# Seven block products for eight in the input projection: Strassen's scheme for keys, queries, values and gates of all tokens, and for conv of the first 768

## The chip, the cores and the metric

The kernel runs on one core of a Trainium2 chip, in one launch. The metric is the device time of one execution in microseconds. The runs of the kernel before have a median of 1464.25 us (1463.36 to 1465.06, three runs).

## The reference, cut to what matters

One layer of a streaming encoder: an input projection to eight groups of 512 columns, a gated short convolution, attention over a band of nine chunks of 64 tokens, an output projection, a gated embedding. All is float32; 2048 prompt tokens and 32 sample tokens go through the same weights.

```python
z = rmsnorm(x, norm_in) @ w_in                # (2080, 1024) @ (1024, 4096)
h, bg, cg, zc, q, k, v, za = split(z, 512)
u  = cg * h
yc = bg * (w[0]*u[t-2] + w[1]*u[t-1] + w[2]*u[t]) * silu(zc)
ya = softmax(q @ k_band.T / 8 + bias) @ v_band * silu(za)     # 8 heads of 64
x  = x + concat(rmsnorm(yc), rmsnorm(ya)) @ w_out
x  = x + sigmoid(rmsnorm(x) @ w_ple_gate) * (p @ w_ple_proj)
return rmsnorm(x), and the newest keys, values and conv rows
```

## The kernel before, in words

**Precision.** Every matrix factor is split into a high part, rounded to the fast float32 format, and a low part, the rest. A product is three matmuls: high by high, high by low, low by high (`products`, L279 to L281; conv has its own copy at L1085). A split is one ACT copy for the high part and one DVE subtraction for the low part.

**Tokens and weights.** The 2080 tokens, normalised and transposed (features on partitions), stay on the chip as `Xh` and `Xl`, in five chunks of 256, 384, 512, 512 and 416 tokens. The 4096 columns of `w_in` come in 16 slots of 256 columns: keys, queries, values, gates (`a`), then eight slots of conv pairs (h with C, B with z). Weights of a slot are loaded to `RAW`, split into `WS` (two sets) while the slot before is multiplied.

**First stage.** For each slot and chunk, `block` makes 24 matmuls (8 k-blocks by 3) into one of five PSUM banks in turn. Keys and queries are split and stored to HBM (`split_store`, L294 to L299), gates go through Silu. Values are made token-major, with tokens as the stationary side, 128 tokens at a time (`values`), so they need no transposes. Of the newest keys token-major rows are wanted too: `key_rows` puts their transposes in a list, `held`, and `release` emits them after the next block. Background work (caches, `w_out` and the two embedding weights, split and stored to `wd`) is done two pieces at a time behind a chunk. Stores are staged in `hi_r` and `lo_r`, three buffers of 512 columns each.

**Conv.** Eight slots for the first pass over tokens (chunks 0 and 1), whose split weights are also stored to `wc`. The passes over chunks 2, 3 and 4 load them again; their matmuls are the dense work between which the pieces of attention are put (`dense`, `attention`, one piece whenever the share of dense columns done passes the share of pieces).

**Output stage.** Output projection, embedding, final norm, per 128 tokens; weights loaded from `wd` in blocks.

All order is written out by hand: each engine runs its instructions in the order of the code, SP issues nearly all DMAs in that order, ACT the loads of background work.

## Time and profile before

| | |
|---|---|
| median of the runs | 1464.25 us |
| profiled execution: its own time | 1465.2 us |
| its span, first to last instruction | 1463.2 us |
| busy: PE, DVE, ACT, POOL | 97%, 42%, 37%, 21% |
| first stage (keys, queries, values, gates) | 11.5 to 400.3 us |
| conv, first pass | 400.3 to 515 us |
| conv with attention | 515 to 1016 us |
| output stage | 1016 to 1463.2 us |

The span is what the queries of the trace count in; about 2 us of the time lie outside it. PE's durations of single matmuls overlap, so what one costs is seen in the distance between starts. A busy time counts an engine only while it computes: waiting and issuing DMAs are left out.

### The profile page before, as it was taken

The numbers are of one execution on the slowest core, as the hardware profiler recorded it, in microseconds if no ns is written. First come the engines' busy times: TensorE is split into PE (matmuls) and PEld (weight loads), VectorE is DVE, ScalarE is ACT, GpSimd is POOL, SyncE is SP. The second block draws the span as 40 slices with busy tenths as digits, with TensorE's granted clock in tenths as the row PEclk, the third lists the DMA queues.
The fourth block names the chain that finished last, engine by engine and source line by source line (L and its number), as shares of the span: only waits on it lengthen the run. The fifth ranks groups of instructions, "written<-read, shape, count | busy, mean of one in ns | idle before, by whom it ended". The sixth has DMA issues, their size and how long they took to land.

```text
span 1463.2 us, 22734 instructions
## 1 busy us (share of the span) xinstructions
PE 1426.2 (97%) x8362; PEld 1269.9 (87%) x8362; DVE 609.4 (42%) x1346; ACT 543.5 (37%) x1182; POOL 314.0 (21%) x438
## 2 busy tenths in 40 slices
...
GB/s 222 196 109 198 294 314 312 292 286 149 79 249 260 213 183 180 159 163 122 170 174 195 126 148 270 251 231 232 363 102 69 72 48 93 48 80 40 60 25 33
DMA packets 176391, 249.10 MB, mean 170 GB/s; under 512 B 19564, under 2 KB 124816, under 8 KB 170136
## 3 DMA queue, kind: packets, MB, share of 16 engines
...
## 4 chain that ended last, share of the span: by engine, by line
PE 86%; DMA 5%; DVE 3%; issue 2%; ACT 2%; SPq 1%; POOL 1%; POOLq 0%; DVEq 0%; ACTq 0%
PE PS L1085 20%; PE PS L279 17%; PE PS L280 16%; PE PS L281 16%; PE PS L546 5%; PE PS L664 3%; PE PS L618 3%; DMA GR<-wd 2%; PE PS L662 1%; PE PS L871 1%; DMA GR<-qs 1%; PE PS L829 1%; PE PS L268 1%; DMA GF<-ext 1%; DVE GF L1099 1%
## 5 line engine op out<-in xcount | busy, mean ns | idle before, releaser
L279 PE MATMUL PS<-GR 128*128 128x512 f32 (+3 forms) x1336 | 476.2, 356 | 2.9 <-DVE GF L1120 1.8
L280 PE MATMUL PS<-GR 128*128 128x512 f32 (+3 forms) x1336 | 471.9, 353 | 1.1 <-DVE GR L271 0.6
L281 PE MATMUL PS<-GR 128*128 128x512 f32 (+3 forms) x1336 | 471.9, 353 | 0.5 <-DVE GR L812 0.5
L1085 PE MATMUL PS<-GR 128*128 128x512 f32 (+3 forms) x1920 | 432.1, 361 | 0.6 <-DMA GR<-wc 0.6
L1085 PEld LDWEIGHTS PS<-GR 128*128 128x128 f32 x1920 | 310.8, 191 | 16.8 <-DMA GR<-wc 0.9
L279 PEld LDWEIGHTS PS<-GR 128*128 128x128 f32 x1336 | 253.2, 190 | 34.2 <-DVE GF L1120 2.1
L281 PEld LDWEIGHTS PS<-GR 128*128 128x128 f32 x1336 | 253.1, 189 | 31.6 <-DVE GR L812 1.0
L280 PEld LDWEIGHTS PS<-GR 128*128 128x128 f32 x1336 | 253.4, 190 | 30.9 <-DMA GR<-wd 1.1
L578 POOL TENSOR_SCALAR GF<-GF,SM 128x640 f32<-128x640 f32 (+3 forms) x132 | 98.5, 746 | 265.7 <-DVE SM L572 195.8
L593 DVE TENSOR_TENSOR GR<-PS,GR 128x256 fp32r<-128x256 f32 (+2 forms) x184 | 103.2, 562 | 98.9 <-ACT GR L592 98.7
L592 ACT ACTIVATE GR<-PS 128x256 fp32r<-128x256 f32 (+2 forms) x184 | 89.8, 489 | 78.4 <-PE PS L618 76.7
L1107 POOL TENSOR_TENSOR GF<-GF 128x512 f32<-128x512 f32 (+3 forms) x20 | 22.4, 1122 | 409.1 <-DVE GF L1106 408.4
L566 ACT ACTIVATE GF<-GF,SM 128x640 f32<-128x640 f32 (+3 forms) x132 | 99.9, 757 | 22.7 <-DVE SM L558 21.4
L558 DVE CUSTOM_DVE_ANT_0 GF<-PS,GF 128x640 f32<-128x640 f32 (+3 forms) x132 | 96.2, 729 | 24.7 <-PE PS L546 20.8
L546 PE MATMUL PS<-GR 128*128 128x320 f32 (+6 forms) x512 | 94.9, 307 | 11.7 <-DMA GR<-qs 7.4
L546 PEld LDWEIGHTS PS<-GR 128*128 128x128 f32 x512 | 81.4, 190 | 20.9 <-issue 7.7
L910 DVE TENSOR_TENSOR GF<-PS,GF 128x512 f32<-128x512 f32 (+2 forms) x35 | 23.6, 675 | 176.3 <-ACT GF L909 176.3
L909 ACT ACTIVATE GF<-PS,SM 128x512 f32<-128x512 f32 (+2 forms) x35 | 23.6, 675 | 163.9 <-PE PS L281 82.7
L664 PE MATMUL PS<-GR 128*128 128x256 f32 x448 | 78.0, 289 | 3.0 <-DVE GR L593 3.0
L195 DVE SCALAR_TENSOR_TENSOR GR<-GF,cT,GR 128x256 fp32r<-128x256 f32 x112 | 45.8, 480 | 73.9 <-ACT GR L194 73.9
L912 POOL TENSOR_TENSOR GF<-GF 128x512 f32<-128x512 f32 (+1 forms) x32 | 41.1, 1285 | 159.7 <-DVE GF L910 141.5
L671 ACT ACTIVATE GF<-PS 64x256 f32<-64x256 f32 (+1 forms) x72 | 26.0, 360 | 130.7 <-PE PS L664 124.2
...
## 6 DMA issues: line engine op xcount, KB each, us to landing
GR<-wc SPq DMA_DIRECT2D x32, 1024.0 KB, 7.3
GR<-wd SPq DMA_DIRECT2D x72, 256.0 KB, 6.8
...
wc<-GR SPq DMA_DIRECT2D x16, 1024.0 KB, 7.6
GR<-qs SPq DMA_DIRECT2D x128, 128.0 KB, 3.2
wd<-GF SPq DMA_DIRECT2D x50, 256.0 KB, 6.1
...
vd<-GF SPq DMA_DIRECT2D x40, 256.0 KB, 5.1
```

What stands on the lines that cost most here:

```text
L195: dve.scalar_tensor_tensor(wl[:, k], RAW[:, k], cT[:, k:k + 1], wh[:, k].bitcast(F32), ALU.mult, ALU.subtract)
L279: pe.matmul(out, wh(k), xh(k), start=(k == ks_[0]), stop=False)
L280: pe.matmul(out, wh(k), xl(k), start=False, stop=False)
L281: pe.matmul(out, wl(k), xh(k), start=False, stop=(k == ks_[-1]))
L546: pe.matmul(ps[:, e, c:c + n_], q[h][b][:, qa], K[h][:, r:r + n_], start=(b == 0 and c == 0), stop=(b == 1), skip_group_check=True)
L558: dve.tensor_tensor_reduce(pr.rearrange("p (b c) -> p b c", b=nb), ps, br.rearrange("p (b c) -> p b c", b=nb), 1.0, 3e38, ALU.add, ALU.min ...
L566: act.activation(pr, pr, AF.Exp, bias=mx[rows], scale=-1.0, accum_out=sm[rows])
L578: pool.tensor_scalar(pr, pr, rs[rows], 1.0, ALU.mult, ALU.mult)
L592: act.activation(dst_of(hi), src, AF.Copy)
L593: dve.tensor_tensor(dst_of(lo), src, dst_of(hi).bitcast(F32), ALU.subtract)
L664: pe.matmul(PS[:, PS_AV, 0:256], v(k), t[:, slot_of[k], :], start=(i == 0), stop=(i == len(both) - 1))
L1085: pe.matmul(ps, a[:, k, js], b[c][:, k, :], start=(k == i == 0), stop=(k == KT - 1 and i == 2))
```

## The change

**The scheme.** For a slot of 256 columns and a pass of 2n tokens, the weights are a 2 by 2 of blocks A (column half by k half) and x a 2 by 2 of blocks B (k half by token half). Strassen's scheme in Winograd's form makes the four result blocks from seven block products, each 12 matmuls (4 k-blocks by 3) of n columns, instead of eight. The factors are A11, A12, A22 and four sums S1 to S4 of weight quarters on one side; B11, B21, B22 and four differences T1 to T4 on the other (`XP`). All seven on each side are split into high and low. The products are steps 0 to 6 of a slot: steps 0, 2, 4, 6 use one PSUM bank, X, and 1, 3, 5 another, Y. ACT copies the first product out after step 0 (L472); DVE adds make U2 after step 1, U4 after step 3 and the blocks C22, C12, C21 after steps 4, 5, 6; step 2 leaves the fourth block, C11, in PSUM.

**Passes.** Three passes over tokens (`PARTS`): 768 to 1535 (n = 384), 1536 to 2079 (n = 272), 0 to 767 (n = 384). Each goes through the eight slots of keys, queries, values and gates: slots 0 to 23. Weights are loaded, summed and split anew in each pass. Slots 24 to 31 are conv for the last pass, tokens 0 to 767. For the other 1312 tokens x is stored, split, to `xd` (`keep_x`), and loaded again as three chunks of 480, 432 and 400 tokens for the conv under attention, which makes 24 matmuls a block as before.

**What goes with it.** Values come out with features on partitions and are transposed. x is no longer on the chip as a whole, only the pass's seven pieces; the pieces of the next pass are split during the eighth slot of a pass. Weight pieces lie in a ring of ten. Staging of stores is one ring, `hl_r`, of three buffers that hold high and low parts (768 columns). Background work is taken one piece at a time, up to three in a slot, after steps 1, 3, 5 (`work_one`), loads after steps 0, 2, 4; none in slots 7, 8, 9, 12, 13 and 23. The first slots' steps are interleaved with the preparation of x.

**Values and newest keys on PE**, in slot 8 (keys of tokens 1536 to 2079; before: keys of chunk 3). Names: PS is PSUM, GR and GRa hold split factors, GF staging, ident the identity of a transpose. Before, around the transposes of one block:

```order
L279 MATMUL PS<-GR 128x512
L280 MATMUL PS<-GR 128x512
L281 MATMUL PS<-GR 128x512
L313 MATMUL PS<-ident,GF 128x128
L279 MATMUL PS<-GR 128x512
L280 MATMUL PS<-GR 128x512
```

Now:

```order
L374 MATMUL PS<-ident,GF 128x128
L374 MATMUL PS<-ident,GF 112x128
L374 MATMUL PS<-ident,GF 32x128
L466 MATMUL PS<-GRa 128x272 x12
L374 MATMUL PS<-ident,GF 128x128
L374 MATMUL PS<-ident,GF 112x128
L374 MATMUL PS<-ident,GF 32x128
```

The transposes (L313, now L374) stood behind the 24 matmuls of the next block; now they stand behind the 12 of the step that makes their block, ahead of the next step, and values have them too.

**Background work and stores on ACT**, in a slot of queries (slot 3; before: the second slot of queries). L294 and L351 write high parts of queries, L336 and L540 those of cache values, L376 those of background weights, L244 those of weights of the next slot, L283 evacuates transposed x; DMA rows load background work. Before:

```order
L294 ACTIVATE GR<-PS 128x416
L294 ACTIVATE GF<-PS 128x416
L336 ACTIVATE GF<-GF 128x4x64 x4
L371 DMA GF<-in_w_out_dram 128x512 x2
L294 ACTIVATE GF<-PS 128x256
L294 ACTIVATE GR<-PS 128x256
L376 ACTIVATE GF<-GF,cT 128x512 x2
L371 DMA GF<-in_w_out_dram 128x512 x2
L294 ACTIVATE GR<-PS 128x384
L294 ACTIVATE GF<-PS 128x384
```

Now:

```order
L283 ACTIVATE ST<-PS,cT 128x128 x4
L244 ACTIVATE GRa<-GF 128x512
L540 ACTIVATE GF<-GF 128x4x64 x2
L351 ACTIVATE GF<-GF 128x384
L244 ACTIVATE GRa<-GF 128x512
L534 DMA GF<-in_cache_v_dram 128x512
L351 ACTIVATE GF<-GF 128x384
L244 ACTIVATE GRa<-GF 128x512
L540 ACTIVATE GF<-GF 128x4x64 x2
L351 ACTIVATE GF<-GF 128x384
L244 ACTIVATE GRa<-GF 128x512 x2
L266 ACTIVATE PS,SM<-ST 128x1024
```

The stores' high parts stood in groups of two to four, each with a PSUM bank of five; now single ones alternate with background work and weight splits, all through the one staging ring.

**The start on DVE**: before, from the first normalised tiles to the first store; now, from the low part of the second piece of x (B21) to that of T2. L209 and L245 make low parts of weights, L271 and L285 evacuate transposed x, L269 normalises, L315 makes low parts of x pieces, L309 differences of x blocks; ST holds x. Before:

```order
L257 TENSOR_SCALAR GF<-GF,SM 128x1024 x2
L209 SCALAR_TENSOR_TENSOR GR<-GF,cT,GR 128x128 x4
L271 TENSOR_TENSOR GR<-PS,GR 128x4x128 x2
L209 SCALAR_TENSOR_TENSOR GR<-GF,cT,GR 128x128 x2
L271 TENSOR_TENSOR GR<-PS,GR 128x4x128 x2
L209 SCALAR_TENSOR_TENSOR GR<-GF,cT,GR 128x128 x2
L246 COPY cT<-PS 128x36
L209 SCALAR_TENSOR_TENSOR GR<-GF,cT,GR 128x128 x8
L295 SCALAR_TENSOR_TENSOR GF<-PS,GF 128x256
```

Now:

```order
L315 TENSOR_TENSOR GRa<-ST,GRa 128x1536
L285 TENSOR_SCALAR ST<-PS,cT 128x128 x4
L245 TENSOR_TENSOR GRa<-GF,GRa 128x512
L269 TENSOR_SCALAR GF<-GF,SM 128x1024
L245 TENSOR_TENSOR GRa<-GF,GRa 128x512
L285 TENSOR_SCALAR ST<-PS,cT 128x128 x4
L269 TENSOR_SCALAR GF<-GF,SM 128x1024
L285 TENSOR_SCALAR ST<-PS,cT 128x128 x4
L309 TENSOR_TENSOR GF<-ST 128x1536
L309 TENSOR_TENSOR ST<-ST,GF 128x1536
L245 TENSOR_TENSOR GRa<-GF,GRa 128x512
L315 TENSOR_TENSOR GRa<-ST,GRa 128x1536
```

Evacuated x was split at once (L271); now it is evacuated whole, and the splits and differences of 1536 elements follow as instructions of their own.

The diff, cut to its core:

```diff
-CHUNKS = [(0, 256), (256, 384), (640, 512), (1152, 512), (1664, 416)]
+PARTS = [(768, 384), (1536, 272), (0, 384)]
+CHUNKS = [(768, 480), (1248, 432), (1680, 400)]
...
-PASSES = [(0, 1), (2, 3), (4,)]
+PASSES = [(0, 1), (2,)]
...
-    hi_r = Ring([G(4132, 512), G(5156, 512), R(O_SP, 512).bitcast(F32)])
-    lo_r = Ring([G(4644, 512), G(5668, 512), R(O_SP + 512, 512).bitcast(F32)])
...
-    psm = Ring([0, 1, 2, 3, 4])
...
+    XP = ["B11", "T2", "B21", "T1", "T3", "B22", "T4"]
+    hl_r = Ring([G(6400 + 768 * i, 768) for i in (2, 0, 1)])
...
+    def sums(q):
...
+        tt(S1, quad(raw, 1, 0), quad(raw, 1, 1), ALU.add)
+        tt(S2, S1, quad(raw, 0, 0), ALU.subtract)
+        tt(S3, quad(raw, 0, 0), quad(raw, 1, 0), ALU.subtract)
+        tt(S4, quad(raw, 0, 1), S2, ALU.subtract)
+
+    def split_w(q, *pieces):
...
+        for i in pieces:
+            hi, lo = piece(q, i)
+            act.activation(hi, src[i], AF.Copy)
+            (pool if i in (4, 5) else dve).tensor_tensor(lo, src[i], hi.bitcast(F32), ALU.subtract)
...
+    def combine(p, name, on=pool):
+
+        a, b = {"T1": ("B12", "B11"), "T2": ("B22", "T1"), "T3": ("B22", "B12"),
+                "T4": ("B21", "T2")}[name]
+        on.tensor_tensor(xsource(p, name), xsource(p, a), xsource(p, b), ALU.subtract)
+
+    def split_x(p, name, on=dve):
+        hi, lo = xpiece(p, XP.index(name))
+        src = xsource(p, name)
+        act.activation(hi, src, AF.Copy)
+        on.tensor_tensor(lo, src, hi.bitcast(F32), ALU.subtract)
...
+    def step(q, i, use, mid=None):
...
+        ps = (X, Y, X, Y, X, Y, X)[i]
...
+        for k in range(4):
+            for m, (a, b) in enumerate(((wh, xh), (wh, xl), (wl, xh))):
+                pe.matmul(ps, a[:, k], b[:, k], start=(first and k == m == 0),
+                          stop=(k == 3 and m == 2), skip_group_check=True)
+            if mid and k == 1:
+                mid()
+        c = lambda t: t[:, 0:n]
+        if i == 0:
+            act.activation(c(t1_of(q)), X, AF.Copy)
+        elif i == 1:
+            dve.tensor_tensor(c(U2), Y, c(t1_of(q)), ALU.add)
+        elif i == 2:
+            use(q, 0, 0, X)
+        elif i == 3:
+            dve.tensor_tensor(c(U4), Y, c(U2), ALU.add)
+        else:
+            out, base, a, j, e = ((C22, U4, X, 1, 1), (C12, U2, Y, 0, 1), (C21, U2, X, 1, 0))[i - 4]
+            dve.tensor_tensor(c(out), a, c(base), ALU.add)
+            use(q, j, e, c(out))
...
+    def token_major(src, p, e, use):
...
+        def later():
+            pt = PS[:, pst()].rearrange("p (a b) -> p a b", a=4)
+            for m, (o, w, _) in enumerate(got):
+                pe.transpose(pt[0:w, m], src[:, o:o + w], ident)
...
+        held.append(later)
...
+    split_x(0, "B11")
+    sums(0)
+    norm_x(9, dve)
+    step(0, 0, take)
+    split_x(0, "B21")
+    tr_x(9)
...
+    combine(0, "T1", dve)
+    combine(0, "T2", dve)
+    split_w(0, 1)
+    split_x(0, "T2")
+    later.pop(0)()
+    constants(cst2, 8, 36)
+    step(0, 1, take)
...
+    def prepare_w(q, i):
+
+        if i == -1:
+            sums(q)
+            split_w(q, 0, 2)
+        elif i == 1:
+            split_w(q, 1, 3)
+        elif i == 3:
+            split_w(q, 6)
+            if NQ <= q < len(SLOTS):
+                keep_w(q)
+            load_raw(q + 1)
+        elif i == 4:
+            split_w(q, 4)
+        elif i == 5:
+            split_w(q, 5)
...
+    def kqva_slot(q):
...
+        for i in range(7):
+            if (q, i) in done:
+                continue
+            step(q, i, take, mid.get(i))
+            release()
+            if s8 == 7 and p < 2:
+                t = XP[i]
+                split_x(p + 1, t)
+                if t in ("B11", "B21", "B22"):
+                    keep_x(p + 1, t)
+                if t == "B21":
+                    combine(p + 1, "T4")
+            prepare_w(q + 1, i)
...
+            if not busy:
+                if i in (1, 3, 5) and len(loaded) == 2:
+                    work_one()
+                if i in (0, 2, 4):
+                    load_one()
```

795 lines of the change are left out of this document (476 added, 319 removed).

## The prediction, made before the change had been run

> **What bounds the kernel now.** I read the page first (busy time, chain), then busy time by stage, then single matmuls.
>
> ```profile
> span 1463.2 us, 22734 instructions
> PE 1426.2 (97%) x8362; PEld 1269.9 (87%) x8362; DVE 609.4 (42%) x1346; ACT 543.5 (37%) x1182; POOL 314.0 (21%) x438
> ...
> PE 86%; DMA 5%; DVE 3%; issue 2%; ACT 2%; SPq 1%; POOL 1%; POOLq 0%; DVEq 0%; ACTq 0%
> ...
> ```
>
> TensorE is busy for 97% of the span and holds 86% of the chain of waits. The next view cuts the span at the places where the program changes; its columns are length, busy time of PE, PEld, DVE, ACT and POOL, granted clock, DMA share and GB/s.
>
> ```profile
> 11.50:400.30 388.80, 387.15 (x2413) 361.42 (x2413) 122.38 (x244) 144.88 (x315) 29.68 (x47) 1.00 0.66 222
> 400.30:515.00 114.70, 114.70 (x779) 114.33 (x778) 42.38 (x100) 33.83 (x81) 7.32 (x11) 1.00 0.68 239
> 515.00:1016.00 501.00, 480.32 (x3098) 429.33 (x3097) 280.05 (x748) 232.86 (x566) 141.87 (x216) 0.99 0.55 186
> 1016.00:1463.20 447.20, 435.80 (x2032) 357.22 (x2030) 160.39 (x243) 124.78 (x205) 132.61 (x154) 0.99 0.27 88
> 150.00:250.00 100.00, 100.00 (x639) 94.50 (x638) 35.88 (x68) 32.48 (x67) 0.00 (x0) 1.00 0.90 310
> ```
>
> The first row is keys, queries, values and gates: 387.15 of 388.80 us of TensorE. The second is conv of the first 640 tokens, the third the rest of conv under attention, the fourth the output stage, which the change leaves alone. In the first two nothing but TensorE matters: DVE and ACT are busy for under 40%, so they may come late without being felt. In the last row, 100 us out of the first stage, DMA is at 0.90 of its time with 310 GB/s and TensorE never waits. So a matmul removed is worth its interval, as long as the others keep up. The price of one is the distance from start to start, not its duration. Single matmuls in order of time (first and last of 14 rows, of 12, of 11):
>
> ```profile
> 20.28 0.28 PE L280 MATMUL PS<-GR 128*128 128x256 f32 x1
> ...
> 21.84 0.28 PE L281 MATMUL PS<-GR 128*128 128x256 f32 x1
> ...
> 34.10 0.33 PE L279 MATMUL PS<-GR 128*128 128x384 f32 x1
> ...
> 36.00 0.34 PE L281 MATMUL PS<-GR 128*128 128x384 f32 x1
> ```
>
> ```profile
> 55.82 0.39 PE L280 MATMUL PS<-GR 128*128 128x512 f32 x1
> ...
> 58.08 0.39 PE L281 MATMUL PS<-GR 128*128 128x512 f32 x1
> ```
>
> So 256 columns cost 1.56/13 = 0.120 us, 384 cost 1.90/11 = 0.173, 512 cost 2.26/10 = 0.226. On the lines between: 272 columns 0.127, 400 0.180, 416 0.186, 432 0.193, 480 0.213.
>
> **The products removed.** Before, a 128-column block of the projection over all tokens is 24 x (0.120 + 0.173 + 2 x 0.226 + 0.186) = 22.3 us; twelve for keys, queries and gates make 269, values (17 tiles x 48 x 0.120) 98: 367 us. Now 24 slots (8 column pairs in 3 passes) have 84 matmuls each: 672 x (0.173 + 0.127 + 0.173) = 318. That is **-49**. Conv's eight Strassen slots take 672 x 0.173 = 116 where the old first pass took 384 x (0.120 + 0.173) = 112.5: **+4** there; but they cover 768 tokens instead of 640, and what is left under attention is 384 x (0.213 + 0.193 + 0.180) = 225 for 384 x (2 x 0.226 + 0.186) = 245: **-20**.
>
> **Transposes and the places where TensorE now waits.** Values now come out feature-major, so each block is transposed: 72 transposes, at
>
> ```profile
> 46.42 0.87 PE PS L268 x8
> ```
>
> 0.87/8 = 0.11 us each: **+8**. They are emitted directly behind the step that makes the block, not one block later as the key transposes were. TensorE runs in order, so it waits there for the DVE add (or ACT copy) and the hand-over. 24 such places in values and 8 in keys, 0.56 us for the add (the 128x384 row below) plus 0.1: **+21**. Below nothing is excluded, since step and transposes depend on each other; above it is whatever DVE is late.
>
> ```profile
> L194 ACT ACTIVATE GR<-GF,cT 128x256 fp32r<-128x256 f32 x112 | 46.2, 497 | 8.8 <-DMA GF<-in_w_in_dram 8.8
> ...
> L195 DVE SCALAR_TENSOR_TENSOR GR<-GF,cT,GR 128x256 fp32r<-128x256 f32 x112 | 45.8, 480 | 73.9 <-ACT GR L194 73.9
> ...
> L912 POOL TENSOR_TENSOR GF<-GF 128x512 f32<-128x512 f32 x30 | 38.6, 1286 | 155.1 <-DVE GF L910 140.3 <-issue 14.7
> ...
> L812 DVE TENSOR_TENSOR GR<-GR 128x1024 fp32r<-128x1024 f32 x16 | 19.6, 1223 | 13.4 <-ACT GR L811 12.1
> ...
> L592 ACT ACTIVATE GR<-PS 128x128 fp32r<-128x128 f32 x16 | 4.3, 266 | 0.0
> ...
> L295 DVE SCALAR_TENSOR_TENSOR GF<-PS,GF 128x384 fp32r<-128x384 f32 x5 | 2.8, 557 | 8.5 <-ACT GF L294 8.5
> ...
> L376 ACT ACTIVATE GF<-GF 128x512 fp32r<-128x512 f32 x3 | 1.9, 627 | 0.5 <-DMA wd<-GF 0.5
> ```
>
> **The start.** Before:
>
> ```profile
> 1.17 4.53 DMA GF<-in_x_prompt_dram
> 5.78 1.16 ACT GF L255 x2
> ...
> 7.29 0.92 POOL SM L144
> ...
> 8.91 1.13 DVE GR L209 x4
> 10.04 1.20 DVE GR L271 x2
> ...
> 12.42 0.38 PE PS L280
> ```
>
> First tile after 5.7 us, first product near 12, then almost no gap. Now step 1 needs three whole token tiles, and four steps (8.3 us of TensorE) can run before T2, which needs all six tiles. Until T2's low part DVE has 6 normalisations and 24 evacuations, 4 weight parts, 2 differences of 1536 and 3 low parts of 1536. At 1.22 for 1024 elements, 0.27 for 128 (ACT's row, taken for DVE too), 0.61 for 512 and 1.83 for 1536 (the 1024 row halved, and by one and a half) that is 7.3 + 6.5 + 2.4 + 9.2 = 25 us, behind the first normalisation at 8.2: 33 at the earliest. Following the queues (the last tiles land behind 5 MB; ACT's squares stand behind its own splits) I get 43. Then each of the next steps needs on DVE an add, a low part for the store, a weight part and a 1.83 us split: 0.56 + 0.56 + 0.61 + 1.83 = 3.6 us and a hand-over against 2.1 of TensorE, so slot 0 ends near 65. Slot 1 adds five weight parts and the storing of B12: 80. TensorE's own work to there is 12 + 29 + 5 = 46; less the 2 us lost before, **+32** (bounds +20 and +40).
>
> **The slots with background work.** This decides. A slot of 384 columns has 84 x 0.173 = 14.5 us of products, of 272 10.7. Every store of keys, queries, gates, values and prepared weights goes through one ring of three staging buffers, written by ACT, then DVE, freed when the store has landed. A slot with three pieces of background work uses it 4 + 6 = 10 times. A use lasts 0.50 (ACT, 256 columns) + 0.48 (DVE) + 0.4 (SP's issue) + landing:
>
> ```profile
> wd<-GF SPq DMA_DIRECT2D x50, 256.0 KB, 6.1
> ...
> GF<-in_w_in_dram SPq DMA_DIRECT2D x6, 1024.0 KB, 6.5
> ...
> kd<-GF SPq DMA_DIRECT2D x12, 192.0 KB, 2.1
> ```
>
> 2.1 us landing gives 3.5 a use, 10/3 x 3.5 = 11.6 a slot, hidden; 6.1 gives 7.5 and 25 us. A loaded slot moves 1.05 (weights) + 0.5 (x) + 1.6 + 1.6 (stores) + 0.8 MB = 5.5 MB, in 18 us 305 GB/s: what the 150 to 250 stretch moves, where the 6.1 belongs; but there stores went out in groups of four to eight, here three at most. I take 4.0: 5.4 a use, **18 us** a slot. By DMA alone 5.5 MB at 310/0.90 GB/s are 16.0, so the slot is over 14.5 in any case. ACT waits in order for the buffer; behind it stand the copy of the first product and the weight splits, and TensorE has two PSUM banks, one step of slack (2.1 us), where it had five. So: six key, query and gate slots of 384 columns (slots 2, 3, 16 to 19) +19 together, value slots 4, 5, 20 +3 (their waits hide most), slot 6 with a flush +5, slots 10, 11, 14 of 272 columns (8 to 12 uses against 11) +13, slot 15, where DVE also has seven splits of 1.8, +7, slot 7 +2: **+49**. The four sums of weight quarters and two low parts, 6 x 1.29 = 7.7 us on POOL, lie beside 10.7 or more; uncovered they would cost the rest of 7.7. Loading weights (6.5 us for 1 MB) lies beside the last three steps.
>
> **Under attention**, the 20 us of dense work saved count nearly in full, TensorE being busy 480 of 501 us, and
>
> ```profile
> L546 PE MATMUL PS<-GR 128*128 128x128 f32 x48 | 10.8, 253 | 7.4 <-DMA GR<-qs 7.4
> ```
>
> the 7.4 us that the first scores waited for queries go, as their load now stands a slot earlier; chunk 1 of x, loaded behind the last slot, gives half of it back: **-24** with the 20.
>
> **Sum**, against the profiled execution's 1465.2 (span 1463.2): -49 + 4 + 8 + 21 + 32 + 49 - 24 = +41, 1506. The median of the runs is 1 lower: **1505 us**.
>
> **The clock.** When TensorE stood still for 2.2 us, the clock was granted at 0.51 for the next 3.5 us:
>
> ```profile
> 774.90:777.10 2.20, 0.00 (x0) 0.00 (x0) 1.97 (x6) 0.00 (x0) 0.00 (x0) 1.00 0.00 0
> 777.70:781.20 3.50, 3.50 (x11) 2.71 (x10) 0.92 (x3) 1.43 (x4) 1.63 (x3) 0.51 0.13 41
> ```
>
> Stalls of 2 us in fourteen slots would cost up to 14 x 1.7 = 24 us; I leave that to the upper bound, since a slot's stall is spread over several steps. [...]
>
> **Rivals.** (1) *Stores land as quietly as the 2.1 us of keys*: the ring never fills, the +49 goes, 1456. For it: only three stores are out at a time; against: the bytes per slot. [...] This case is faster; it turns at a landing of about 3 us. (2) *TensorE stays the only bound*, start and waits hidden too: 1465 - 49 + 4 - 24 + 8 = 1404. For it: DVE and ACT are below 45% on average; against: the start has no other work. (3) *Landing at 6.1, and the clock falls at the stalls*: 25 us for ten loaded slots and more in the short ones, +85 on the forecast at the end, 1550 in its middle. (4) Start and waits just eat what the products save: 1465. That the products are not made fewer is excluded: the program has 84 a slot.
>
> **Chances.** Forecast (1475 to 1535) 0.57; rival 1 0.15, rival 2 0.06, rival 3 0.17, rival 4 0.05 (its higher half counts as the same). Range 1435 to 1555: it takes in rival 1 and most of rival 3, and leaves out rival 2 and the tail of 3. A change within 0.2% cannot be told from none here: faster 0.22, same 0.03, slower 0.75.
>
> **What would show it.** TensorE busy below 85% between 80 us and the last gate slot; ACT's longest waits on stores of weights, keys and queries; loaded slots of 384 columns 17 to 20 us long, against 14.5 to 16 in conv's slots; the first product on T2 after 33 us; the first dense matmul of conv near 580 us (now 515). If loaded slots take 15 to 16 us, the ring was priced wrong and rival 1 holds; if slot 1 ends before 60 us, the start was.

## The result, and the profile after

The changed kernel takes **1753.26 us** (median of four runs, 1750.91 to 1754.42) against 1464.28 of the kernel before in the same rounds: 1.197 times as long (95% interval 1.195 to 1.199). The forecast was 1505, with 1555 as its upper end: slower as said, but by 289 us instead of 41.

The head of the page and the first line of the chain of waits of the changed kernel:

```profile
span 1752.6 us, 23444 instructions
PE 1467.5 (84%) x8102; PEld 1318.3 (75%) x8102; DVE 903.5 (52%) x1669; ACT 679.7 (39%) x1465; POOL 631.0 (36%) x640
...
PE 53%; DMA 10%; DVE 6%; issue 5%; ACT 4%; POOL 2%; SPq 1%; ACTq 0%; DVEq 0%; POOLq 0%
```

TensorE held 86% of the chain and holds 53% now. It has 260 matmuls fewer, but is busy for 41 us more. The next view says why: busy time by stage (slots 0 and 1; slots 2 to 23; conv's Strassen slots up to the first dense matmul; conv with attention; output stage), columns as in the prediction.

```profile
23.30:121.10 97.80, 54.34 (x202) 47.56 (x203) 52.62 (x62) 33.85 (x62) 33.79 (x25) 0.67 0.35 118
121.10:668.00 546.90, 371.71 (x2041) 351.45 (x2040) 318.34 (x482) 232.90 (x528) 239.52 (x173) 0.85 0.60 185
668.00:810.60 142.60, 128.92 (x675) 122.91 (x674) 89.26 (x115) 43.46 (x80) 73.74 (x54) 0.93 0.69 223
810.60:1300.00 489.40, 462.58 (x3109) 429.60 (x3107) 275.10 (x747) 234.18 (x568) 141.09 (x221) 0.99 0.60 201
1300.00:1752.60 452.60, 439.85 (x2028) 358.25 (x2028) 160.18 (x243) 123.97 (x205) 133.84 (x154) 0.99 0.26 87
```

In the first two rows the granted clock is 0.67 and 0.85, where it was 1.00. In stretches granted 0.50, 259 us long in all before the dense conv, TensorE is busy for 158 us; a step's 12 products, 2.1 us at 0.173 each, took 4.21 us in one of them (from 65.37 us). So its busy time grows. Nobody else is full either: of 546.9 us DVE is busy for 58%, ACT for 43%, POOL for 44%, DMA at 0.60. It is a stage in which everyone waits for someone. Against the forecast's times: slots 0 and 1 end at 121 us (80 was said, +41); slots 2 to 23 take 547 (580 less 80 less 116 of conv: 384, +163); conv's slots 142 (116, +26); the rest 943 (the 948 of before less 24, +19). Together that is, to a microsecond of rounding, the whole error of 248. (Conv's slots end here at the first dense matmul, at 810.5 us; the expectations count that point some 3 us earlier, as 807.)

TensorE's groups in these stages, with what ended its idle time; L472 is the copy of the first product, L474 the add of U2, L314 a high part of x, L481 the adds of C22, C12, C21:

```profile
L466 PE MATMUL PS<-GRa 128*128 128x384 f32 (+1 forms) x2688 | 528.4, 358 | 174.1 <-ACT GF L472 95.4 <-DVE GF L474 21.5 <-ACT GRa L314 18.6
...
L374 PE MATMUL PS<-ident,GF 128*128 128x128 f32 (+3 forms) x96 | 19.1, 313 | 50.1 <-DVE GF L481 42.6 <-ACT GF L441 6.9 <-issue 0.6
```

The products waited 174 us, most for the copy; the transposes 50, where the forecast had 21. One of the waits for the copy, in slot 17 ahead of its third step, in order of time. SP's rows are DMA issues; what stands in brackets is how long the engine had been idle, and for whom:

```profile
507.62 0.37 SPq L204 DMA_DIRECT2D GF<-in_w_in_dram  x1
508.62 2.22 SPq L508 DMA_DIRECT2D wd<-GF  x2
...
516.21 0.52 ACT L351 ACTIVATE GF<-GF 128x384 fp32r<-128x384 f32 x1 [4.16 <-DMA wd<-GF]
...
518.55 0.51 ACT L504 ACTIVATE GF<-GF,cT 128x256 fp32r<-128x256 f32 x1 [0.50 <-DMA kd<-GF]
...
519.09 1.19 DVE L505 SCALAR_TENSOR_TENSOR GF<-GF,cT 128x256 fp32r<-128x256 f32 x1 [0.21 <-ACT GF L504]
...
520.20 0.55 DVE L481 TENSOR_TENSOR GF<-PS,GF 128x384 f32<-128x384 f32 x1
520.83 0.52 ACT L351 ACTIVATE GF<-GF 128x384 fp32r<-128x384 f32 x1 [1.77 <-DVE GF L481]
521.26 0.61 ACT L244 ACTIVATE GRa<-GF 128x512 fp32r<-128x512 f32 x1
...
522.30 0.47 ACT L472 ACTIVATE GF<-PS 128x384 f32<-128x384 f32 x1
...
522.82 1.01 PE L466 MATMUL PS<-GRa 128*128 128x384 f32 x2 [5.30 <-ACT GF L472]
```

Read it upwards. TensorE waits 5.30 us for the copy. Ahead of the copy on ACT stand weight splits (L244) and the store of C21 (L351), which waits for DVE's add, which stands behind DVE's low part of background work (L505), which waits for ACT's high part (L504). That one waited half a microsecond for a staging buffer, and stands on ACT behind the store of the block before (L351 at 516.21), which had waited 4.16 us for one: that buffer came free when a store of background weights landed, over 7 us after its issue, with the load of 1 MB of weights issued 1 us ahead of it. Which of these links carries the time is what the runs ask.

### The profile page after: what moved, and what is told of

It is laid out like the page before. It is cut to its first block, busy times and chain, and to the rows that moved or that the text cites. A ratio compares the mean times of both kernels' runs of the same rounds, so it can differ in the third digit from the quotient of the medians.

```text
span 1752.6 us, 23444 instructions
## 1 busy us (share of the span) xinstructions
PE 1467.5 (84%) x8102; PEld 1318.3 (75%) x8102; DVE 903.5 (52%) x1669; ACT 679.7 (39%) x1465; POOL 631.0 (36%) x640
## 4 chain that ended last, share of the span: by engine, by line
PE 53%; DMA 10%; DVE 6%; issue 5%; ACT 4%; POOL 2%; SPq 1%; ACTq 0%; DVEq 0%; POOLq 0%
PE PS L1401 10%; PE PS L466 8%; PE PS L1161 7%; PE PS L1160 7%; PE PS L1159 7%; PE PS L882 4%; PE PS L1000 3%; PE PS L954 2%; DMA wd<-GF 2%; DMA qs<-GF 2%; PE PS L998 1%; DMA GRa<-wd 1%; DVE GRa L245 1%; DMA kd<-GF 1%; PE PS L1214 1%
## 5 line engine op out<-in xcount | busy, mean ns | idle before, releaser
L466 PE MATMUL PS<-GRa 128*128 128x384 f32 (+1 forms) x2688 | 528.4, 358 | 174.1 <-ACT GF L472 95.4
L466 PEld LDWEIGHTS PS<-GRa 128*128 128x128 f32 x2688 | 494.2, 213 | 195.5 <-ACT GF L472 100.7
L245 POOL TENSOR_TENSOR GRa<-GF,GRa 128x512 fp32r<-128x512 f32 x64 | 86.4, 1351 | 337.7 <-ACT GRa L244 337.7
L1401 PE MATMUL PS<-GRa 128*128 128x432 f32 (+1 forms) x768 | 189.5, 366 | 0.4 <-DMA GRa<-wc 0.4
L245 DVE TENSOR_TENSOR GRa<-GF,GRa 128x512 fp32r<-128x512 f32 x160 | 164.3, 1057 | 33.2 <-ACT GRa L244 32.9
L1160 PE MATMUL PS<-GRa 128*128 128x512 f32 (+1 forms) x440 | 170.3, 387 | 1.0 <-DMA GRa<-wd 1.0
L1159 PE MATMUL PS<-GRa 128*128 128x512 f32 (+1 forms) x424 | 164.1, 387 | 1.8 <-DMA GRa<-wd 1.3
L1161 PE MATMUL PS<-GRa 128*128 128x512 f32 (+1 forms) x424 | 163.8, 386 | 0.0
L244 ACT ACTIVATE GRa<-GF 128x512 fp32r<-128x512 f32 x224 | 131.7, 619 | 82.2 <-DMA GF<-in_w_in_dram 29.1
L929 DVE TENSOR_TENSOR GRa<-PS,GRa 128x256 fp32r<-128x256 f32 (+2 forms) x184 | 103.1, 563 | 93.5 <-ACT GRa L928 92.4
L1401 PEld LDWEIGHTS PS<-GRa 128*128 128x128 f32 x768 | 131.0, 191 | 3.2 <-DMA GRa<-wc 0.8
L928 ACT ACTIVATE GRa<-PS 128x256 fp32r<-128x256 f32 (+2 forms) x184 | 89.7, 488 | 70.5 <-PE PS L954 69.1
L882 PE MATMUL PS<-GRa,GRb 128*128 128x320 f32 (+6 forms) x512 | 95.0, 308 | 16.4 <-DVE SM L894 12.4
L1401 PE MATMUL PS<-GRb,GRa 128*128 128x480 f32 x384 | 107.8, 397 | 0.0
L1160 PEld LDWEIGHTS PS<-GRa 128*128 128x128 f32 x440 | 82.8, 188 | 18.7 <-DMA GRa<-wd 1.7
L1159 PEld LDWEIGHTS PS<-GRa 128*128 128x128 f32 x424 | 79.6, 188 | 19.5 <-DMA GRa<-wd 2.1
```

What stands on the lines that cost most here:

```text
L244: act.activation(hi, src[i], AF.Copy)
L245: (pool if i in (4, 5) else dve).tensor_tensor(lo, src[i], hi.bitcast(F32), ALU.subtract)
L466: pe.matmul(ps, a[:, k], b[:, k], start=(first and k == m == 0), stop=(k == 3 and m == 2), skip_group_check=True)
L882: pe.matmul(ps[:, e, c:c + n_], q[h][b][:, qa], K[h][:, r:r + n_], start=(b == 0 and c == 0), stop=(b == 1), skip_group_check=True)
L929: dve.tensor_tensor(dst_of(lo), src, dst_of(hi).bitcast(F32), ALU.subtract)
L1159: pe.matmul(out, wh(k), xh(k), start=(k == ks_[0]), stop=False)
```

## The experiments

Each run is one edit of the changed kernel and one time (two runs of the changed kernel differ by up to 3.5 us). The kernel before took 1461.3 to 1465.3 us beside them. Stage lengths are from the starts of the slots' first matmuls, and up to the first dense matmul for conv's slots. In runs whose edit does not touch conv's slots these spread from 142 to 145 us, so 2 or 3 us in a stage of a single run show nothing by themselves:

| edit | time | slots 0, 1 end | slots 2 to 23 | conv's slots |
|---|---|---|---|---|
| none (changed kernel) | 1753 | 121 | 547 | 142 |
| weight loads on another queue | 1765 | 121 | 560 | 143 |
| five staging buffers | 1733 | 120 | 526 | 145 |
| background work behind slot 23 | 1814 | 122 | 472 | 274, with that work |
| background work without stores in the slots, all of it again behind slot 23 | 1855 | 120 | 515 | 273, with that work |
| POOL's work left out, raw weights held longer | 1772 | 123 | 551 | 156 |
| POOL's work left out | 1713 | 120 | 522 | 128 |
| weight splits behind the copy | 1781 | 121 | 575 | 139 |
| weight splits and C21's store behind it | 1755 | 119 | 554 | 141 |
| third bank | 1745 | 121 | 543 | 143 |
| transposes a step later | 1744 | 120 | 535 | 143 |
| start's splits a step earlier | 1739 | 104 | 547 | 144 |
| idle matmuls in the waits, first dose | 1769 | 129 | 556 | 142 |
| idle matmuls in the waits, half the dose | 1741 | 116 | 541 | 143 |
| no preparation of x in slots 8 to 13 | 1735 | 120 | 529 | 145 |
| four edits together | 1695 | 103 | 511 | 142 |
| four edits, sums on DVE | 1687 | 104 | 509 | 137 |
| four edits, POOL's work left out | 1647 | 106 | 479 | 124 |

### Is it the stores and the staging ring?

Theory Q: the prediction's term, stores that land late, with the weight load ahead of them on SP's queue as the reason. Three runs:

```diff
-            sp.dma_start(raw, win[:, c:c + 256]...)
+            (pool if q > 2 else sp).dma_start(raw, win[:, c:c + 256]...)
```

> The 1 MB weight loads from slot 3 on are issued from POOL's queue instead of SP's, nothing else. Theory Q (a staging buffer is held because its store lands behind the weight load in SP's queue; ACT then waits in order, the first product's copy comes late, TensorE stands): the slots of keys and queries in the last pass, 22.5 us now, fall to 18 or less, the stores that followed a weight load land in 2 to 3 us instead of 7, total 1690 to 1710. Theory P (DVE instructions with two operands in SBUF are slowed by POOL's; DVE comes late): those slots stay within 1 us of 22.5, total within 10 us of 1753.

```diff
+    bg_r = Ring([G(10112 + 512 * i, 512) for i in range(2)])
...
-                hl = hl_r()[:, 0:512]...
+                hl = hl_bg()[:, 0:512]...
...
+        apart[0] = q in (4, 5, 10, 11, 16, 17, 18, 19, 20, 21, 22)
```

> Background work gets two staging buffers of its own in slots 4, 5, 10, 11 and 16 to 22; three stay for the products' stores. Theory Q: key and query slots of the last pass fall from 22.5 to 17 to 19 us, total 1700 to 1720. Theory P: they stay within 1 us of 22.5.

```diff
-        busy = q in (7, 8, 9, 12, 13, 23)
+        busy = True
...
+    while todo or loaded:
+        load_one()
+        load_one()
+        work_one()
```

> No background work in slots 0 to 23; all 44 pieces are done in one stretch behind slot 23, ahead of conv. Theory Q: slots 2, 3 and 16 to 19 take 15 to 17 us (22 now), the clock there is granted at 0.95 or more; the stretch alone takes 88 uses of the ring, 110 to 180 us, so the total stays near 1753. Theory P: DVE's low parts of 512 stay near 1.06 us and those slots above 19 us.

Measured: another queue 1765, no gain (slots 17 to 19 take 23.2 us each, 22.5 before). This run does not clear the queue, though: on POOL's queue the loads themselves landed later (8.5 us after their issue in the median, 6.6 on SP's; the one issued at 523.07 us released its first reader at 531.00), and ACT waited for stores in slots 16 to 19 as long as before (27 us); when the stores landed, its trace does not tell. Five buffers 1733, 20 us less, with slots 17 to 19 between theory and rival (20.9 us). Background work behind slot 23 1814, where the work by itself takes some 130 us. Of the six slots that the theory named, 17 to 19 fell to 15.4 us there; 2, 3 and 16 took 20 to 23 without any background work, so something else holds those. In that run slots 2 to 22 take 441 us instead of 530. A fourth run splits these 89 us, with loading and computing in the slots, and all pieces once more, with their stores, behind slot 23:

```diff
-                sp.dma_start(wd[:, m * 128:(m + 1) * 128, c:c + 256]..., hl)
+                if real[0]: sp.dma_start(wd[:, m * 128:(m + 1) * 128, c:c + 256]..., hl)
...
+    real[0] = True
+    todo.extend(todo0)
```

> In the slots background work is loaded and split on ACT and DVE into the staging ring as in the changed kernel, but not stored; all 44 pieces are done again, with their stores, in a stretch of their own behind slot 23 (as in the run that had them there alone, whose slots 17 to 19 took 15.4 us with no background work at all). So slots 16 to 22 have the computing without the stores. Theory Q (stores that land late hold ACT): slots 17 to 19 take 15.4 to 17 us instead of 22.5. Rival W (ACT's and DVE's own work and its order hold the copy): 19 us or more.

Slots 17 to 19 of the four, each a row of the view by stretches: the changed kernel,

```profile
513.20:580.80 67.60, 50.73 (x254) 48.94 (x253) 40.88 (x60) 27.10 (x54) 24.19 (x19) 0.87 0.76 237
```

five buffers,

```profile
501.70:564.40 62.70, 49.05 (x255) 47.51 (x254) 36.39 (x61) 26.77 (x55) 24.28 (x19) 0.92 0.82 261
```

computing without stores,

```profile
487.50:544.80 57.30, 49.05 (x253) 48.10 (x253) 37.55 (x60) 26.09 (x55) 23.48 (x19) 0.91 0.63 201
```

and no background work:

```profile
464.10:510.40 46.30, 45.21 (x254) 43.53 (x253) 34.74 (x42) 18.95 (x36) 26.16 (x19) 1.00 0.63 197
```

A slot takes 22.5, 20.9, 19.1 and 15.4 us. So half of what background work costs is there without a single one of its stores, although ACT is busy for 9 of the 19 us and DVE for 12.5; the other half goes with the stores (their issue, their traffic and their landing, which this run does not tell apart). Over slots 2 to 22 the same: 441, 484 without stores, 530. Between theory Q (15.4 to 17) and its rival (19 or more) the run falls on the rival's side for the slot, but leaves Q its half.

### DVE beside POOL

L245 (a low part of 512 columns) took 1.06 us on average, and one difference of 1536 columns in the start 4.78, against the 0.61 and 1.83 of the prediction. A kernel by itself ran DVE's kinds eight times each beside POOL's two-input adds, POOL's one-input operations and an idle POOL; it computes nothing of the layer and its outputs are zeros:

```python
pool_two(26)    # pool.tensor_tensor(GP[:, 0:512], GP[:, 1024:1536], GP[:, 2048:2560], ALU.add)
for i in range(8):
    dve.tensor_tensor(c(i % 7, 512), GA[:, 0:512], GB[:, 512:1024], ALU.subtract)
for i in range(8):
    dve.tensor_tensor(c(i % 7, 512), PS[:, 0], GB[:, 512:1024], ALU.subtract)
for i in range(8):
    dve.scalar_tensor_tensor(c(i % 7, 256), GA[:, 0:256], Z[:, 0:1], GB[:, 512:768], ...)
for i in range(8):
    dve.tensor_scalar(c(i % 7, 512), GA[:, 0:512], 2.0, None, ALU.mult)
```

> No projection at all: outputs are filled with zeros, and DVE runs four kinds of instruction eight times each, three times over: POOL idle, POOL busy with two-input additions of 512 elements, POOL busy with one-input multiplications of 1024. Theory P: DVE's subtraction of 512 with both operands in SBUF takes 0.6 to 0.7 us with POOL idle and 1.0 or more beside POOL's additions; with one operand in PSUM it takes 0.69 in every case; the one-input kind does not change. If all kinds stay within 10% in the three cases, the 1.06 us in the changed kernel has another cause.

POOL did not wait between the phases, so its adds ran beside the first block of DVE's operations, and the third block had POOL idle from about 100 us on. Minimum, median and maximum in ns, and first and last start, of POOL's adds and of DVE's operations in the first and the third block:

```profile
L117 POOL TENSOR_TENSOR GP<-GP x26: 1263/1323/1704, 24.0 to 60.8; 128x512 f32<-128x512 f32 x26
...
L125 DVE TENSOR_TENSOR GC<-GA,GB x8: 677/1743/1743, 23.3 to 32.8; 128x512 f32<-128x512 f32 x8
...
L127 DVE TENSOR_TENSOR GC<-PS,GB x8: 678/678/691, 34.6 to 38.8; 128x512 f32<-128x512 f32 x8
...
L129 DVE SCALAR_TENSOR_TENSOR GC<-GA,Z,GB x8: 490/1478/1479, 39.5 to 48.3; 128x256 f32<-128x256 f32 x8
...
L131 DVE TENSOR_SCALAR GC<-GA x8: 1369/1478/1480, 49.8 to 59.5; 128x512 f32<-128x512 f32 x8
...
L145 DVE TENSOR_TENSOR GC<-GA,GB x8: 677/681/1520, 96.1 to 102.9; 128x512 f32<-128x512 f32 x8
...
L149 DVE SCALAR_TENSOR_TENSOR GC<-GA,Z,GB x8: 476/477/483, 108.5 to 111.3; 128x256 f32<-128x256 f32 x8
...
L151 DVE TENSOR_SCALAR GC<-GA x8: 419/421/426, 111.8 to 114.1; 128x512 f32<-128x512 f32 x8
```

Two inputs in SBUF: 681 ns alone, 1743 beside POOL. 256 columns: 477 and 1478. One input in SBUF: 421 and 1478. With one input in PSUM nothing happens (678 beside POOL, 682 alone). Theory P had the two-input and the PSUM kind right and missed the one-input kind, which was to stay as it is. POOL's own adds hardly suffer (1263 at best, 1323 in the median). Each of the three SBUF kinds took 1001 to 1062 ns longer beside these adds; what holds DVE there was not shown.

Does it carry the 250 us? Two runs left POOL's weight sums out.

```diff
     def sums(q):
+        return
...
-        src = [quad(raw, 0, 0), SUM[:, 1], quad(raw, 0, 1), SUM[:, 0], SUM[:, 2], SUM[:, 3], ...
+        src = [quad(raw, 0, 0), quad(raw, 1, 0), quad(raw, 0, 1), quad(raw, 1, 0), quad(raw, 0, 0), ...
...
-            (pool if i in (4, 5) else dve).tensor_tensor(lo, src[i], hi.bitcast(F32), ALU.subtract)
+            dve.tensor_tensor(lo, src[i], hi.bitcast(F32), ALU.subtract)
```

> Leaves out the four sums of weight quarters on POOL (the pieces S1 to S4 take plain quarters, so the output is not the reference's) and puts the low parts of two of them on DVE instead of POOL: POOL does nothing in slots 16 to 23 but the DMA issues. The same products, splits, stores and loads stay. Theory P (DVE operations with both operands in SBUF are slowed by POOL: 0.68 to 1.74 us for 512 columns in the run that measured it alone): the 512-column low parts of weights go from a mean of 1.06 to about 0.7 us, the 256-column low parts of background work from 0.83 to about 0.5, DVE is busy for some 60 us less although it has 64 parts more; TensorE's waits for DVE before the dense conv (about 95 us) fall by a third or more, the copies of the first product come earlier too: dense conv starts at 730 to 770 us instead of 807, time 1675 to 1715. Rival O (the waits come from the order in the queues and from stores that land late; DVE has slack anyway): the DVE rows fall the same, but dense conv starts at 785 or later, time above 1730.

It took 1772. The reason is a second change that the edit brought with it: splits 4 and 5 read the raw weights instead of the sums, so the next load could start only two steps later, and ACT waited for it in front of the copy (135.9 us now, 29.1 in the changed kernel):

```profile
L245 ACT ACTIVATE GRa<-GF 128x512 fp32r<-128x512 f32 x224 | 131.6, 620 | 169.4 <-DMA GF<-in_w_in_dram 135.9 <-PE PS L467 32.4 <-ACT GF L473 1.1
```

The second run keeps the raw weights' release where it was:

```diff
     def sums(q):
+        if q > 1:
+            return
...
-            (pool if i in (4, 5) else dve).tensor_tensor(lo, src[i], hi.bitcast(F32), ALU.subtract)
+            dve.tensor_tensor(lo, src[i], hi.bitcast(F32), ALU.subtract)
```

> The weight sums on POOL are left out from slot 2 on (the pieces S1 to S4 are split from the stale sums of slot 1, so the output is not the reference's), and the low parts of two pieces are on DVE instead of POOL; the buffer of raw weights comes free at the same step as in the changed kernel, which was not so in the run without POOL work above, where splits read it two steps longer. Theory P (slow DVE operations beside POOL): DVE's 512-column low parts 0.73 us as there, conv slots 15 to 16 us instead of 15 to 23, dense conv 30 us or more earlier than 807. Rival W: the DVE rows fall, but the waits for the copy of the first product stay above 80 us and dense conv starts less than 20 us earlier.

1713, 40 us less. The low parts, changed kernel and this run:

```profile
L245 DVE TENSOR_TENSOR GRa<-GF,GRa 128x512 fp32r<-128x512 f32 x160 | 164.3, 1057 | 33.2 <-ACT GRa L244 32.9
...
L505 DVE SCALAR_TENSOR_TENSOR GF<-GF,cT 128x256 fp32r<-128x256 f32 x64 | 51.1, 825 | 25.8 <-ACT GF L504 21.5 <-DMA zd<-GF 4.1
```

```profile
L247 DVE TENSOR_TENSOR GRa<-GF,GRa 128x512 fp32r<-128x512 f32 x224 | 156.1, 722 | 61.7 <-ACT GRa L246 60.7
...
L507 DVE SCALAR_TENSOR_TENSOR GF<-GF,cT 128x256 fp32r<-128x256 f32 x64 | 32.1, 527 | 8.4 <-ACT GF L506 8.4
```

As theory P had it, the operations go from 1057 to 722 and from 825 to 527 ns, and conv's slots lose 14 of their 26 us too many. Those 14 us are not DVE's speed alone: without the sums ACT does not wait for them either, which in conv's slots of the changed kernel it did for 21.9 us. The rest of the gain is in slots 2 to 23 (25 us, 11 of them in slot 14, where POOL's queue had been busy for 20 of 23 us with differences of x and sums). A real cost, then, but a sixth of the whole.

### Is it the order in the queues, or too few banks?

Theory W: the copy is late for what stands ahead of it on ACT. So that was put behind it, in two stages; the second run has the first edit too.

```diff
-        prepare_w(q + 1, -1)
...
         for i in range(7):
...
             step(q, i, take, mid.get(i))
+            if i == 0:
+                prepare_w(q + 1, -1)
```

> The sums of the next slot's weights and the splits of its pieces 0 and 2 stand behind step 0 and its copy, instead of ahead of step 0, in slots 2 to 31; the same instructions. Theory W (the copy of the first product is late because it stands in ACT's queue behind splits that wait for the weights to land and for POOL's sums; TensorE waited 95 us for it before the dense conv, 19 times): the waits for the copy fall to about 55 us, the conv slots lose theirs (7 us) altogether, dense conv starts 30 to 45 us earlier than 807, time 1705 to 1725. Rival R (ACT is late from stores that land late, and waits for the buffer ahead of the copy all the same): less than 15 us gained, the waits for the copy stay above 80 us.

```diff
-            step(q, i, take, mid.get(i))
+            step(q, i, put_last if i == 6 else take, mid.get(i))
+            while i == 0 and last_take:
+                last_take.pop(0)()
```

> As the run before, and the storing of the seventh step's block (C21) stands behind step 0 of the next slot and its copy as well, so that on ACT nothing of the slot before but background work is ahead of the copy. Theory W: waits for the copy below 30 us, dense conv at 720 to 745, time 1660 to 1685. Rival R: less than 25 us gained against the changed kernel, since the waits for staging buffers move to the other steps.

1781 and 1755: W falls. In the second run TensorE's waits are these:

```profile
L466 PE MATMUL PS<-GRa 128*128 128x384 f32 (+1 forms) x2688 | 532.5, 359 | 164.4 <-DVE GF L474 54.3 <-ACT GF L472 42.3 <-ACT GRa L314 18.6
...
L374 PE MATMUL PS<-ident,GF 128*128 128x128 f32 (+3 forms) x96 | 19.0, 312 | 61.4 <-ACT GF L441 29.3 <-DVE GF L481 28.6 <-issue 3.5
```

The wait for the copy fell from 95 to 42, the waits for U2 rose from 21.5 to 54 and for the copy of a block to be transposed from 7 to 29. The wait moved and kept its size. The same with the transposes:

```diff
-            step(q, i, take, mid.get(i))
-            release()
+            due = held[:]
+            held.clear()
+            step(q, i, take, mid.get(i))
+            for f in due:
+                f()
```

> The transposes of values and newest keys stand behind the step after the one that makes their block, instead of directly behind that one; nothing else is changed. Theory T (32 places where TensorE waits in order for DVE's add, 43 us, and for ACT's copy, 7 us, each followed by half clock): the waits before transposes fall below 15 us, value slots of 384 columns go from 35 to 38 us to about 28, dense conv starts 35 to 60 us earlier, time 1695 to 1720. Rival (the block's store and the copies are late anyway, and the next step's wait takes the place): less than 15 us gained.

```profile
L466 PE MATMUL PS<-GRa 128*128 128x384 f32 (+1 forms) x2688 | 535.4, 361 | 190.3 <-ACT GF L472 113.2 <-DVE GF L474 24.6 <-ACT GRa L314 18.6
...
L374 PE MATMUL PS<-ident,GF 128*128 128x128 f32 (+3 forms) x96 | 17.3, 292 | 22.9 <-DVE GF L481 21.8 <-ACT ST L283 0.9
```

Of 50 us before transposes 27 went, but the products wait 16 us longer: 1744, 10 less. And more slack:

```diff
-        ps = (X, Y, X, Y, X, Y, X)[i]
+        seven = (X, Y, X, Y, X, Y, X)
+        if q >= 14:
+            Z = PS[:, 6 + q % 2, 0:n]
+            seven = (X, Y, X, Z, Y, Z, Y)
+        ps = seven[i]
...
-        for i in range(7):
+        for pos, i in enumerate((0, 1, 3, 2, 4, 5, 6) if q >= 14 else range(7)):
```

> From slot 14 on a slot has three PSUM banks instead of two (two banks that only the normalisation of x used, in turn) and its steps run in the order 0, 1, 3, 2, 4, 5, 6: step 3 goes to the third bank, so the copy of the first product has two steps' time before step 2 adds to its bank, and the fourth product's add has two before step 5. The same instructions, the same stores. Theory B (TensorE stalls because two banks leave one step of slack, 2.1 us, while ACT and DVE are free half of the time): waits for the copy vanish from slot 14 on, slots 16 to 19 take 80 us or less instead of 94, the conv slots 126 to 132 instead of 143, time 1710 to 1730. Rival R (the cycle of ACT, DVE and staging buffers itself takes 20 us or more in a slot with background work): the waits move to other steps, slots 16 to 19 stay above 88, time 1735 or more.

1745; slots 16 to 19 took 95 us (94 before), conv's slots 143. Theory B falls: with twice the time for the copy, a loaded slot is as long. What fits this is that one round through ACT, DVE and the ring takes longer than the slot's products, so that no slack on TensorE's side helps; that is inferred, since no run times the round by itself.

### The start, the clock, and the preparation of x

Slot 0 in the changed kernel, one step to the next (L481 adds, L351 stores, L314 and L315 split the next piece of x):

```profile
77.33 0.56 DVE L481 TENSOR_TENSOR GF<-PS,GF 128x384 f32<-128x384 f32 x1 [3.98 <-PE PS L466]
77.92 0.52 ACT L351 ACTIVATE GF<-GF 128x384 fp32r<-128x384 f32 x1 [9.67 <-DVE GF L481]
...
78.87 1.47 ACT L314 ACTIVATE GRa<-ST 128x1536 fp32r<-128x1536 f32 x1
...
80.37 2.78 DVE L315 TENSOR_TENSOR GRa<-ST,GRa 128x1536 fp32r<-128x1536 f32 x1 [1.34 <-ACT GRa L314]
...
83.20 3.89 PE L466 MATMUL PS<-GRa 128*128 128x384 f32 x11 [2.34 <-DVE GRa L315]
...
87.13 0.56 DVE L481 TENSOR_TENSOR GF<-PS,GF 128x384 f32<-128x384 f32 x1 [3.98 <-PE PS L466]
```

From add to add 9.8 us, and every piece of it in series: ACT splits the next x only after it has stored the block of the step before. Written one step earlier:

```diff
-    step(0, 1, take)
     split_w(0, 3)
     split_x(0, "T1")
     combine(0, "T3")
+    step(0, 1, take)
+    split_w(0, 4, 6)
+    split_x(0, "T3")
+    load_raw(2)
...
     step(0, 3, take)
-    split_w(0, 4, 6)
-    split_x(0, "T3")
+    split_w(0, 5)
+    split_x(0, "B22")
...
-    load_raw(2)
```

> In slot 0 alone each split of weights and of x is written one step earlier, ahead of the step whose results stand before it on ACT and DVE; the same instructions. Theory S (in the start each step waits in order for the step before: 4.0 us of products at half clock, DVE's add 0.56, ACT's high part for the store 0.52, ACT's high part of the next x piece 1.47, DVE's low part 1.75, together 8.3 us, which is what stands between the steps in the trace): steps 3 to 6 of slot 0 come 4 to 5 us apart instead of 8, slots 0 and 1 end at 101 to 109 us instead of 121, time 12 to 20 us less, 1733 to 1741. Rival (DVE itself is the bound in the start, or the gain is eaten by the wait for the weights of slot 2): slots 0 and 1 end later than 115.

Slots 0 and 1 end at 104 instead of 121, as theory S had it; 1739. (The load of slot 2's weights moved up with the splits.) As for the clock, matmuls that nothing uses were put into the waits:

```diff
+    def warm(n):
+        for _ in range(n):
+            pe.matmul(PS[:, 6, 0:128], ident, ident, start=True, stop=True)
```

> Matmuls of 128 columns that nothing uses (0.107 us each at full clock) stand ahead of the steps at which TensorE waits: 70 ahead of step 1 of slot 0, 30 ahead of its steps 3, 4, 5 and 6, 40 ahead of step 2 of slots 14 to 21. All other work stays. Theory C (half clock after a stall doubles the products that follow: 158 us of TensorE's busy time before the dense conv is at half clock, so 79 us are lost, 19 of them from 23 to 121 us and 20 in slots 14 to 21): in the start steps of slot 0 take 2.1 us instead of 4.0, slots 0 and 1 end near 112 instead of 121; slots 14 to 19 are granted 0.95 or more instead of 0.81 to 0.92 and become 1 to 2 us shorter each although TensorE has 4.3 us of extra work in each; time 10 to 25 us less. Rival I (the clock costs little, since a faster step only waits longer for the next operand): the granted clock rises all the same, but the slots keep their lengths or grow, time 1745 to 1775.

That run took 1769. The 40 matmuls written into a slot stand in its trace as 80 of 9.09 us together (541.30 to 564.80 us), 0.23 us for each one written instead of 0.107, and TensorE is busy for all 23.50 us of that slot: the added work itself bound the slots. With half the dose (30 ahead of step 1 of slot 0, 15 ahead of steps 3 to 6, 20 ahead of step 2 of slots 16 to 19):

> As the run with idle matmuls, with half the dose and fewer places, since each of its matmuls turned out to be two passes of 0.107 us and so filled more than the waits: 30 ahead of step 1 of slot 0 (6.4 us, wait 8.4), 15 ahead of its steps 3, 4, 5, 6 (3.2 us), 20 ahead of step 2 of slots 16 to 19 only (4.3 us, wait about 5.4 in each). Theory C (half clock after a stall costs time of its own): slots 0 and 1 end at 108 to 116 us instead of 121, slots 16 to 19 take 86 to 90 us together instead of 94 and are granted 0.97 or more. Rival I (a faster step only waits longer for ACT and DVE): slots 16 to 19 stay within 2 us of 94 and the start within 3 us of 121 although the clock rises.

Slots 16 to 19 in the changed kernel and in this run:

```profile
486.80:580.80 94.00, 67.63 (x338) 65.20 (x337) 57.52 (x82) 38.48 (x74) 36.24 (x25) 0.85 0.72 223
```

```profile
477.30:573.50 96.20, 82.72 (x497) 78.76 (x497) 57.75 (x82) 38.48 (x74) 36.33 (x25) 0.96 0.73 225
```

The clock rises from 0.85 to 0.96 and the slots take 96 us instead of 94: rival I. In the start it gave 5 us (116 instead of 121), where theory C's 108 to 116 is just missed and the rival's 3 us are exceeded. The other 6 us by which slots 2 to 23 came out shorter lie mostly in slots 2 to 15, which the edit leaves alone, so they prove nothing. In slots 16 to 19 a step at half clock filled time that TensorE would else have waited: the 158 us of busy time at half speed that the changed kernel's trace shows before the dense conv are not 79 us lost.

The forecast gave nothing to the preparation of the next pass's x. Without it in slots 8 to 13:

```diff
-    x_at.update({8 + j: j for j in range(6)})
```

> The six token tiles of the last pass are not loaded, normalised or transposed in slots 8 to 13: the pass takes what the pass before left in the buffer of x, so the output is not the reference's. All else stays: products, splits of x, weights, stores, background work. In the changed kernel slots 8 to 13 (272 columns, 10.7 us of products each) take 155 us together; the prediction put nothing there for the preparation of x. Theory X (the preparation of the next pass's x, 1 square and 4 evacuations on ACT, 4 evacuations on DVE, 8 transposes between products, normalisation on POOL, is what makes these slots long): slots 8 to 13 take 100 to 125 us, time 1720 or less. Rival (stores, background work and transposes make them long, x preparation fits beside): 140 or more, time above 1735.

The six slots took 136 us instead of 155, between the theory (up to 125) and its rival (140 or more): 19 us, of some 91 that they take beyond their products.

### Do the causes add?

The edits of five buffers, third bank, later transposes and earlier start in one kernel, and then with the edit that left POOL's sums out (the second one) besides:

> Four edits together, all with the full computation: the start's splits one step earlier (alone: 15 us less), transposes one step later (10 less), two more staging buffers for background work in eleven slots (20 less), and the third bank of the run beside this one. If each edit removes a cause of its own, the gains add: 45 us and what the banks gain, 1680 to 1700. If they take the same wait away, or it moves: 1710 or more.

> The run with the four edits, and besides without POOL's weight sums from slot 2 on (pieces S1 to S4 from stale sums, so the output is not the reference's) and with the two low parts of POOL on DVE, which alone gained 40 us. If the causes add: 40 us below the run with the four edits, 1640 to 1660, with dense conv starting near 700. If POOL's part is hidden once the banks give slack: within 15 us of it.

1695 and 1647. The first is 58 below the changed kernel, where the four gains alone add to 15 + 10 + 20 + 8 = 53; the second 48 below the first, where POOL's share alone was 40. So these are separate causes, not one wait counted several times. And the sums on DVE, with the full computation:

```diff
-        tt = pool.tensor_tensor
+        tt = dve.tensor_tensor
```

> The run with the four edits (1695), and the four sums of weight quarters and two low parts are done on DVE instead of POOL, with the full computation: POOL is idle in slots 16 to 23, DVE has six operations of 512 columns more in each slot, 4.1 us at the 0.68 us that one takes with POOL idle. If POOL's slowing of DVE and its own queue cost as much as the run without sums says (48 us), and DVE has room: 1660 to 1685. If DVE's queue is as tight as its hand-overs suggest: 1690 or more.

1687: 8 of the 48 us. DVE's low parts are as fast there as without the sums (746 and 529 ns for 512 and 256 columns), but six more operations a slot now stand in DVE's queue. So the speed beside POOL could not be had for itself: most of POOL's share was work that has to be done somewhere. This is the fastest variant with the full computation, and it is 15% behind the kernel before.

## Why the prediction was wrong

**Right**: the direction; that the products are no longer the bound; their price (without background work slots 17 to 19 take 15.4 us for 14.5 of products); TensorE below 85% up to the last gate slot (371.71 of 546.90 us, 68%). ACT's longest waits on stores of weights, too: the first and a later row of what it waits for in slots 2 to 23 (us in total, times, longest):

```profile
ACT GF L351 <- DMA wd<-GF: 28.8, 6, 6.5
...
ACT GF L504 <- DMA wd<-GF: 12.0, 16, 1.4
```

All its waits for stores there add to 99 us, 64 of them for background weights (`wd`), beside 108 us for DVE and 77 for TensorE; for weights to land it waits only in conv's slots, 29 us. Half right: loaded slots of 384 columns took 22.5 us and not 17 to 20; the first product on T2 came at 57 us, after 33 as said, but 43 was meant.

The error of 248 us, by terms: the start +41, background work +40 (89 for 49), slots 2 to 16 without background work +117, the later slots without it +6, conv's slots +26, the rest +19. (The waits before transposes, 50 for 21, lie inside the slots' terms.)

**The loaded slots (+49)**: this step failed, and not in size alone. It priced a slot by the throughput of one resource, ten uses of a ring of three, and took everything else as hidden beside it. With the landings that the changed kernel shows over its whole run (2.2 to 3.4 us in the median, rows below) its own formula gives 12 to 16 us a slot; the slots took 22.5. The stores are half of what background work costs (47 of 89 us in slots 2 to 22); the other 42 come from its loading and computing, on engines that are busy for less than two thirds of the slot. The reading that fits is a round of hand-overs, ACT to DVE to ACT, in two queues that each keep their order: every late item delays all behind it on its own engine, and through them the other. For it speaks that moving items within the queues moved the wait and shortened it little, for the copy, the transposes and the banks; no run measured the round itself.

**Slots with x work and short slots** had no term beyond products and transposes, and this is the larger miss. Without background work slots 17 to 22 took 99.5 us, where the forecast had about 95 (three of 14.5, two of values at 18 to 19, one of 14.5). Slots 2 to 16 took 342 there, where it had 225 (384 less slot 23, the 49 and these 95). So some 117 us lie in the slots that prepare x or have 272 columns, in which seven weight splits and four stores have to fit beside 10.7 us of products. In that run TensorE stood for 90 of the 342 us, and no single wait holds them: 24 for the copy of the first product, 28 for blocks to be transposed, 26 for DVE's adds ahead of products, 12 for tiles of x from POOL. And it was granted 0.86 of its clock:

```profile
122.30:464.10 341.80, 251.28 (x1414) 236.45 (x1413) 207.84 (x286) 149.21 (x337) 189.79 (x131) 0.86 0.43 133
```

The prediction counted ring uses there, and no hand-overs.

**DVE's durations** came from a stage in which POOL is busy for 29.68 of 388.80 us; now it is busy for 239.5 of 546.9. The 0.61 us for 512 columns were 1.06, the 1.83 of a difference 4.78. Worth 40 to 48 us together with POOL's own queue and the work of the sums itself. Two rows of before might have been a hint, though no run shows that they have this cause; 384 columns took as long as 512:

```profile
L1099 DVE SCALAR_TENSOR_TENSOR GF<-GF,cwh 128x512 f32<-128x512 f32 x16 | 13.3, 832 | 2.3 <-ACT GF L1097 2.1
L1099 DVE SCALAR_TENSOR_TENSOR GF<-GF,cwh 128x384 f32<-128x384 f32 x16 | 13.2, 822 | 0.6 <-ACT GF L1097 0.2
```

**The start (+32)**: bounds of 20 and 40, measured +73. Of the 41 us too many, 14 were there at the first product on T2. The price of a step, 3.6 us, was DVE's work; but the step is a series, since ACT's split of x stands behind the store of the block before. Writing it earlier gave back 17 us, full clock 5.

**Serial waits (+21)** measured 50 us, but taking them away gained 10, since the next wait was behind them.

**Under attention (-24)** came out as -12 (501.0 to 489.4 us): TensorE's busy time there fell by 18 us (480.32 to 462.58) and its idle time rose by 6 (20.7 to 26.8). The output stage, which the change leaves alone, took 5 us more (447.2 to 452.6). No run followed either.

**The clock** was left to the upper bound with 24 us. It was at half far more often, for 158 us of busy time before the dense conv, but with the clock raised (0.96 for 0.85 in slots 16 to 19) the slots kept their length (96 us for 94): it is a symptom more than a cause. In conv's Strassen slots no wait was longer than 2 us, and still the clock fell to 0.50, in stretches of 3.4, 6.8 and 10.2 us. One wait and what came after it:

```profile
726.66:728.64 1.98, 0.00 (x1) 0.00 (x0) 1.68 (x3) 1.93 (x4) 0.70 (x1) 1.00 1.08 380
729.20:732.60 3.40, 3.22 (x11) 2.71 (x9) 3.37 (x3) 1.15 (x2) 3.32 (x3) 0.50 1.05 407
```

In these rows the clock is granted at 0.50 for 3.40 us, from 0.56 us behind a wait of 1.98 us; in the prediction's it was 0.51 behind one of 2.20 us.

**Rivals**: (1) had the landing right for the median store (last column, us from issue to landing, in the changed kernel), and the slots were long all the same. (3) had late stores and half clock, and 200 us too little; (2) and (4) fall by the time alone.

```profile
wd<-GF SPq DMA_DIRECT2D x72, 256.0 KB, 2.2
...
kd<-GF SPq DMA_DIRECT2D x16, 384.0 KB, 2.5
...
qs<-GF SPq DMA_DIRECT2D x16, 384.0 KB, 3.4
```

**Open**: with all that was found taken away (1647), the dense conv starts at 709 us, 129 later than forecast. Where in slots 2 to 16 the remaining time goes, beyond the 19 us of x preparation in six of them, is settled only as far as the waits above: what makes each of them late is open.
